# A two-part transformer on one core: attention heads emitted by pairs instead of one by one

## The chip, the cores and the metric

The kernel runs on one core of one Trainium2 chip. TensorE (PE) multiplies matrices into banks of PSUM, VectorE (DVE), ScalarE (ACT) and GpSimd (POOL) work element by element, SyncE (SP) issues the DMA of the weights. The metric is the device time of one execution in microseconds; lower is better. The kernel before took 1622.57 us, the median of three runs (1611.64 to 1628.34).

## The reference, cut to what matters

256 tokens of 1024 numbers go through two blocks. The first has two layers: differential attention and an expert layer of 64 experts, then multi-head latent attention and a second expert layer. The second block modulates, runs a hybrid mixer of two kinds of attention side by side, and a convolutional gated MLP. All is float32. The parts that the change touches:

```python
def mla_attention(...):                 # 8 heads; q and k of a head: 128 plain + 64 rotated numbers
    ...
    sc = einsum('bqhd,bkhd->bhqk', qb, k) * 192 ** -0.5      # plain part + rotated part
    p = causal_softmax(sc, blk, s)
    return einsum('bhqk,bkhd->bqhd', p, v)                   # v of a head: 128

def swa_attention(q, k, v, sinks):      # 8 window heads of 64, 2 heads of k and v
    scores = q k^T / 8 - slope(h) * dist, masked to a window of 128
    p = exp(scores - m);  probs = p / (sum(p) + exp(sink - m));  out = probs v

def forgetting_attention(q, k, v, f_logit):   # 8 heads of 64
    F = cumsum(log_sigmoid(f_logit))
    s = q k^T / 8 + (F[query] - F[key]);  p = softmax(causal(s));  out = p v
```

## The kernel before, in words

Tokens lie in two tiles of 128 partitions. Weights stream into 19 regions of 8 KB per partition by a plan that is worked off in a fixed order as regions come free (`Regions.fill`, SyncE's queue). Projections are made exact enough by splitting both operands into a rounded part and a rest (ScalarE L412, VectorE L413) and multiplying three times (`mm3`, L428 to L430); these operands are of the type that TensorE takes in one pass, while plain float32 matmuls appear in the trace as two records, one for each pass.

A head of attention has two stages. `stage_a`, `swa_a`, `fox_a` transpose q and k, multiply them into scores (a `sc` bank, of which there are two), and call `probs`: VectorE adds the mask or bias and takes row maxima (L599, L601), ScalarE exponentiates with row sums (L629), VectorE divides (L635, L637). `stage_b`, `swa_b`, `fox_b` call `probsT`, three transposes of the probabilities (L609) into an `at` bank (two of these) and a copy (L611), multiply with v, and split the result into `oT`. `staged(n, ...)` emits the stages of successive items interleaved; a `None` among the stages delays the next one by one item.

In the latent attention (L1281 to L1313) each head has four score matmuls: 128 and then 256 columns, each of them a product over all 128 rows (L1299, L1301) and one over the 64 rotated numbers (L1300, L1302). A pair of heads shares the transposed rotated parts in one tile `pq`, head c in partitions 64c to 64c+63; there is one `pq` for all pairs. A window head has two score matmuls over 64 rows (L1410, L1411). A forgetting head (`fox`) has its two (L1435, L1437), each followed by a bias matmul (L1436, L1438): a column of the identity over 8 rows, repeated to 128 columns, times the negated sums `nfT`. The values of window and forgetting heads come from `av` (L1397, L1398), 64 result partitions for each head, two heads in one bank.

The order on each engine comes from a scheduler that weighs what is ready; SyncE's is the program's. It puts weight matmuls of other projections (L428 to L430) between the heads' work: in the first half of the latent attention those of the second half, in the window heads those of q, k and v of the forgetting heads, in the forgetting heads the first part of the output projection (`out_proj`), all of which need VectorE and ScalarE for splits.

Of the kernel before, what the change touches and what calls it, by code (L numbers as in the profile page):

```python
# [19 lines left out]
P = 128  # L20
# [215 lines left out]
def tile_model(ctx: ExitStack, tc: tile.TileContext, a: dict, out: bass.AP, stop: int = 6):  # L236
# [39 lines left out]
    def phase(*shapes):  # L276

        room, o, out = sp.tile([P, 1152], F32, tag="phase", name="phase", bufs=1), 0, []
# [3 lines left out]
        assert o <= 1152  # L282
        return out
# [515 lines left out]
    def router_weights(i):  # L799

        room, = phase((1152,))
# [358 lines left out]
    def mla():  # L1160
# [35 lines left out]
        rt, kpe, pq = phase((2, T, 2, 64), (T, 64), (512,))  # L1196
# [19 lines left out]
        for i in range(2):  # L1216
# [64 lines left out]
            def stage_a(h, qp=qp, kp=kp, qn=qn, kn=kn, qs=qs, nqs=nqs):  # L1281
                if h % 2 == 0:
                    pt = at_ps()
                    for t in range(T):
                        PE.transpose(pt[:, ts(t, P)], qp[:, t, h:h + 2, :].rearrange("p a b -> p (a b)"), ident)
                        PE.transpose(pt[:, 256 + 128 * t:384 + 128 * t],
                                     kp[:, t, h:h + 2, :].rearrange("p a b -> p (a b)"), ident)
                    V.tensor_copy(pq, pt)
                pt = at_ps()
                for t in range(T):  # L1290
                    PE.transpose(pt[:, ts(t, P)], qn[:, t, h, :], ident)
                    PE.transpose(pt[:, 256 + 128 * t:384 + 128 * t], kn[:, t, h, :], ident)
                qT = t1((256,))
                kT = t1((256,))
                S.activation(qT, pt[:, 0:256], AF.Copy)
                V.tensor_scalar(kT, pt[:, 256:512], gqk[:, 0:1], None, op0=ALU.mult)
                ps = sc_ps()
                rsl = slice(64 * (h % 2), 64 * (h % 2) + 64)
# [6 lines left out]
            def stage_b(h, vv=vv, i=i):  # L1305
                pT = probsT(state[h])
                po = at_ps()
                PE.matmul(po[:, 0:256], lhsT=vv[:, 0, h, :], rhs=pT[:, 0:256], start=True, stop=False,
                          skip_group_check=True)
                PE.matmul(po[:, 128:256], lhsT=vv[:, 1, h, :], rhs=pT[:, 256:384], start=False, stop=True,  # L1310
                          skip_group_check=True)
                split_to(oT[0][:, 4 * i + h, :], oT[1][:, 4 * i + h, :], po[:, 0:256])
            staged(4, stage_a, None, stage_b)  # L1313
# [24 lines left out]
    def mixer():  # L1338
# [3 lines left out]
        kd, va, nfT = phase((T, 4, 64), (T, 2, 64), (256,))  # L1342
        nfT = nfT[0:8, :]
# [30 lines left out]
        PE.matmul(pf[:, 8:16], lhsT=ones, rhs=fl[:, 0, :], start=False, stop=True)  # L1374
        fc = sb([P, T, 8], "fc")
        V.tensor_copy(fc, pf[:, 0:16].rearrange("p (t h) -> p t h", t=2))
        pf2 = at_ps()
        for t in range(T):
            PE.transpose(pf2[0:8, ts(t, P)], fc[:, t, :], ident)
        V.tensor_scalar(nfT, pf2[0:8, 0:256], -8.0, None, op0=ALU.mult)  # L1380
# [14 lines left out]
        def av(po, c, v0, v1, pT):  # L1395
            rs_ = slice(64 * c, 64 * c + 64)
            PE.matmul(po[rs_, 0:256], lhsT=v0, rhs=pT[:, 0:256], start=True, stop=False, skip_group_check=True)  # L1397
            PE.matmul(po[rs_, 128:256], lhsT=v1, rhs=pT[:, 256:384], start=False, stop=True, skip_group_check=True)  # L1398

        def swa_a(h):  # L1400
            hp, c = divmod(h, 2)
            kv = hp // 2
            if h % 4 == 0:
                state["kT"] = pair_T(lambda t: kd[:, t, 2 * kv:2 * kv + 2, :].rearrange("p a b -> p (a b)"))
            if c == 0:
                state["qT"] = pair_T(lambda t: qa[:, t, ts(hp, P)])
            qT, kT = state["qT"], state["kT"]
            rsl = slice(64 * c, 64 * c + 64)
            ps = sc_ps()
            PE.matmul(ps[:, 0:128], lhsT=qT[rsl, 0:128], rhs=kT[rsl, 0:128], start=True, stop=True)  # L1410
            PE.matmul(ps[:, 128:384], lhsT=qT[rsl, 128:256], rhs=kT[rsl, 0:256], start=True, stop=True)  # L1411
            bias = t1((256,))
            G.tensor_scalar(bias, dist, -8.0 * 2.0 ** (-8.0 * (h + 1) / 8), None, op0=ALU.mult)
            state[h] = probs(ps, bias[:, 128:256], bias, 0.125, -0.125,
                             sink=bc("sinks", 8)[:, h:h + 1])

        def swa_b(h):
            hp, c = divmod(h, 2)
            if c == 0:
                state["po"] = at_ps()  # L1420
            pT = probsT(state[h])
            av(state["po"], c, va[:, 0, hp // 2, :], va[:, 1, hp // 2, :], pT)
            if c == 1:
                split_to(oT[0][:, hp, :], oT[1][:, hp, :], state["po"][:, 0:256])

        def fox_a(h):
            hp, c = divmod(h, 2)
            if c == 0:
                state["fqT"] = pair_T(lambda t: qb[:, t, ts(hp, P)])
                state["fkT"] = pair_T(lambda t: kb[:, t, ts(hp, P)])  # L1430
            qT, kT = state["fqT"], state["fkT"]
            rsl = slice(64 * c, 64 * c + 64)
            eh = ident[0:8, h:h + 1].to_broadcast([8, P])
            ps = sc_ps()
            PE.matmul(ps[:, 0:128], lhsT=qT[rsl, 0:128], rhs=kT[rsl, 0:128], start=True, stop=False)  # L1435
            PE.matmul(ps[:, 0:128], lhsT=eh, rhs=nfT[:, 0:128], start=False, stop=True)  # L1436
            PE.matmul(ps[:, 128:384], lhsT=qT[rsl, 128:256], rhs=kT[rsl, 0:256], start=True, stop=False)  # L1437
            PE.matmul(ps[:, 128:384], lhsT=eh, rhs=nfT[:, 0:256], start=False, stop=True)  # L1438

            state[h] = probs(ps, cmask, fmask, 0.125, -0.125)  # L1440

        def fox_b(h):
            hp, c = divmod(h, 2)
            if c == 0:
# [169 lines left out]
```

## Time and profile before

| | us |
|---|---|
| median of 3 runs | 1622.57 |
| lowest, highest | 1611.64, 1628.34 |
| profiled execution | 1618.73 |
| its span | 1616.9 |
| TensorE, VectorE, ScalarE busy in it | 1338.3, 690.5, 434.3 |
| heads of the latent attention, from | 686 to 744 |
| window heads | 1279.7 to 1324.1 |
| forgetting heads | 1339.7 to 1396.6 |

All prices are read from the one profiled execution. A matmul's shown duration contains time in which the next one already runs, so a price is the distance from one start to the next. [...]

### The profile page before, as it was taken

The page shows a single profiled execution, that of the slowest core. Times are in us where ns is not written, and L with a number is a line of the kernel's source. Part 1 is how long each engine was busy: PE and PEld are TensorE (multiplying, and loading weights), DVE is VectorE, ACT ScalarE, POOL GpSimd, SP SyncE. Part 2 cuts the span into 40 slices and gives each one's busy share as a digit, 9 for nine tenths or more (in the row PEclk, how much of TensorE's full clock was granted, in tenths as well). Part 3 has the DMA queues.
Part 4 walks back from the last instruction along what each step waited for, and adds up shares of the span by engine and source line. Part 5 has one row for each costly group of instructions (what it writes and reads, how often), then busy time and mean ns, then how long its engine had stood idle before and what let it go on. Part 6 is the DMA issues. An engine that isn't in the chain of part 4 may idle for free. (4 is left out here: it accounts for less than half of the span.)

```text
span 1616.9 us, 26717 instructions
## 1 busy us (share of the span) xinstructions
PE 1338.3 (83%) x10695; PEld 933.2 (58%) x10695; DVE 690.5 (43%) x1630; ACT 434.3 (27%) x946; POOL 53.5 (3%) x73
## 2 busy tenths in 40 slices
PE   7998987777677777998877777778785999999996
PEld 6766655544443444776644544545452666699996
DVE  6875232222222223875222222222323654477776
ACT  5754010000000001764000000000102443465554
POOL 2110000000000000110000000000000100000001
PEclk9998999898899988999989898898987998899998
DMA  9377889999999997227999999999899763575500
GB/s 365 124 301 326 348 352 417 419 419 417 419 419 418 418 419 295 92 107 314 393 418 418 418 419 418 418 419 388 348 419 368 266 228 114 177 256 180 176 34 27
DMA packets 109020, 513.03 MB, mean 317 GB/s; under 512 B 9875, under 2 KB 37331, under 8 KB 57552
## 3 DMA queue, kind: packets, MB, share of 16 engines
q1 hardware_dynamic: 107280, 507.42, 78.7%
q8 instruction: 160, 2.62, 0.7%
q0 software_dynamic: 1248, 2.00, 0.4%
q14 instruction: 108, 0.88, 0.1%
q10 hardware_dynamic: 224, 0.10, 0.0%
HBM read 508.43 MB, written 1.05 MB: 315 GB/s over the span
## 5 line engine op out<-in xcount | busy, mean ns | idle before, releaser
L981 PE MATMUL ad<-R,t 128*32 128x256 f32 x4096 | 299.1, 411 | 87.5 <-DMA R<-in_moe_w_up_dram 36.5
L981 PEld LDWEIGHTS ad<-R,t 128*32 128x32 f32 x4096 | 157.9, 118 | 233.3 <-issue 71.8
L936 PE MATMUL sc<-t,R 128*128 128x128 f32 x1024 | 169.4, 334 | 7.6 <-issue 7.4
L936 PEld LDWEIGHTS sc<-t,R 128*128 128x128 f32 x1024 | 161.4, 247 | 8.9 <-issue 8.2
L1031 DVE TENSOR_TENSOR x<-x,mm 128x512 f32<-128x512 f32 x140 | 90.0, 684 | 147.8 <-PE mm L1028 147.8
L987 ACT ACTIVATE t<-ad 128x256 f32<-128x256 f32 x32 | 12.3, 383 | 440.2 <-PE ad L981 440.2
L1008 PE MATMUL mm<-R,t 128*32 128x512 f32 x1024 | 120.0, 610 | 9.3 <-PEq L1072 5.9
L422 ACT ACTIVATE t<-mm,ws 128x512 fp32r<-128x512 f32 x64 | 44.0, 687 | 262.7 <-PE mm L1008 262.6
L413 DVE TENSOR_TENSOR R<-R,R 128x1024 fp32r<-128x1024 f32 (+3 forms) x78 | 90.9, 1169 | 33.5 <-ACT R L412 32.3
L989 DVE TENSOR_TENSOR t<-t,ad 128x256 f32<-128x256 f32 x32 | 13.5, 421 | 212.8 <-ACT t L987 212.8
L413 DVE TENSOR_TENSOR t<-R,t 128x1024 fp32r<-128x1024 f32 (+3 forms) x76 | 89.5, 1182 | 22.2 <-ACT t L412 22.0
L938 DVE TENSOR_TENSOR t<-sc,ffng 128x512 f32<-128x512 f32 x64 | 44.3, 692 | 126.9 <-PE sc L936 126.9
L960 PE MATMUL at<-con,t 128*128 128x128 f32 x64 | 16.0, 340 | 96.9 <-PEq L1108 90.3
L412 ACT ACTIVATE R<-R 128x1024 fp32r<-128x1024 f32 (+3 forms) x78 | 78.7, 1013 | 52.8 <-PE ad L430 20.2
L423 DVE SCALAR_TENSOR_TENSOR t<-mm,ws,t 128x512 fp32r<-128x512 f32 x64 | 48.1, 751 | 101.9 <-ACT t L422 75.1
L1028 PE MATMUL mm<-t,t 128*128 128x512 f32 x256 | 77.7, 423 | 11.1 <-DVE x L1031 10.2
L412 ACT ACTIVATE t<-R 128x1024 fp32r<-128x1024 f32 (+3 forms) x76 | 76.5, 1009 | 32.8 <-PE ad L429 13.2
L1008 PEld LDWEIGHTS mm<-R,t 128*32 128x32 f32 x1024 | 30.9, 112 | 73.6 <-issue 70.0
L960 PEld LDWEIGHTS at<-con,t 128*128 128x128 f32 x64 | 7.4, 162 | 110.3 <-issue 104.4
L1028 PEld LDWEIGHTS mm<-t,t 128*128 128x128 f32 x256 | 43.1, 188 | 45.2 <-DVE x L1031 22.9
L428 PE MATMUL mm<-R,R 128*128 128x512 f32 (+3 forms) x139 | 56.3, 408 | 2.6 <-ACT R L412 2.6
L429 PE MATMUL mm<-R,R 128*128 128x512 f32 (+3 forms) x139 | 55.9, 403 | 0.5 <-DVE R L413 0.5
(472 smaller groups left out, 2346.6 us busy)
## 6 DMA issues: line engine op xcount, KB each, us to landing
R<-in_moe_w_gate_dram SPq DMA_DIRECT2D x128, 1024.0 KB, 19.7
R<-in_moe_w_up_dram SPq DMA_DIRECT2D x128, 1024.0 KB, 18.8
R<-in_moe_w_down_dram SPq DMA_DIRECT2D x128, 1024.0 KB, 19.8
R<-in_w_ada_dram SPq DMA_DIRECT2D x24, 1024.0 KB, 7.7
R<-in_w_up_dram SPq DMA_DIRECT2D x22, 1024.0 KB, 6.2
R<-in_diff_w_in_dram SPq DMA_DIRECT2D x12, 1024.0 KB, 13.3
R<-in_w_down_dram SPq DMA_DIRECT2D x11, 1024.0 KB, 6.5
R<-in_w_in_dram SPq DMA_DIRECT2D x8, 1024.0 KB, 8.0
```

The lines of the kernel that those rows point to most:

```text
L412: S.activation(hi, w, AF.Copy)
L413: V.tensor_tensor(lo, w, hi.bitcast(F32), op=ALU.subtract)
L422: first = S.activation(hi, src, AF.Copy, scale=scale)
L423: V.scalar_tensor_tensor(lo, src, scale, hi.bitcast(F32), op0=ALU.mult, op1=ALU.subtract)
L428: PE.matmul(acc, lhsT=lt[0], rhs=rt[0], start=start, stop=False, **kw)
L429: PE.matmul(acc, lhsT=lt[0], rhs=rt[1], start=False, stop=False, **kw)
L936: PE.matmul(pg[:, ts(k4, P)], lhsT=h[:, t, 4 * hb + k4, :], rhs=gm[:, t].rearrange("p a b -> p (a b)"), start=(t == 0), stop=(t == 1))
L938: V.tensor_tensor(xg[hb], pg.rearrange("p (k n) -> p k n", k=4), gain[:, 4 * hb:4 * hb + 4, None].to_broadcast([P, 4, P]), op=ALU.mult)
L981: mm = PE.matmul(pgu[32 * j:32 * j + 32, co:co + 256], lhsT=xg[k // 4][:, k % 4, 32 * j:32 * j + 32], rhs=w, start=(k == 0 and co == 0), s ...
L1008: mm = PE.matmul(py[32 * j:32 * j + 32, :], lhsT=hT2[:, k, 32 * j:32 * j + 32], rhs=ws[j][:, k, ts(hf, 512)], start=(k == 0), stop=(k == 1))
L1028: PE.matmul(pos[t], lhsT=sc[:, ts(t, P)], rhs=y[part], start=(part == 0), stop=(part == 1))
L1031: V.tensor_tensor(xs, xs, pos[t], op=ALU.add)
```

## The change

Latent attention, window heads and forgetting heads go through `staged` by pairs of heads. A pair's scores are emitted column block by column block, both heads in turn, into two banks; the values likewise, both heads' 256 columns and then both heads' 128. In the latent attention the `None` between the stages is dropped, and `pq` is taken from a ring of slots for each pair. The sums of the forgetting bias are split into a rounded part and a rest, which stand in 16 rows of a one-pass type; the bias matmul multiplies them with a selector `e16` that has two ones in a column. The shared tile `phase` shrinks from 1152 to 768 numbers.

```diff
-            def stage_a(h, ...):
-                if h % 2 == 0:
-                    pt = at_ps()
...
-                    V.tensor_copy(pq, pt)
...
-                PE.matmul(ps[:, 0:128], lhsT=qT[:, 0:128], rhs=kT[:, 0:128], start=True, stop=False)
-                PE.matmul(ps[:, 0:128], lhsT=pq[rsl, 0:128], rhs=pq[rsl, 256:384], start=False, stop=True)
-                PE.matmul(ps[:, 128:384], lhsT=qT[:, 128:256], rhs=kT[:, 0:256], start=True, stop=False)
-                PE.matmul(ps[:, 128:384], lhsT=pq[rsl, 128:256], rhs=pq[rsl, 256:512], start=False, stop=True)
-                state[h] = probs(ps, cmask, fmask, qs[:, :, h], nqs[:, :, h])
+            def stage_a(hp, ...):
+                pq = t2((512,))
...
+                pss = [sc_ps(), sc_ps()]
+                for t, sl in QT:
+                    n = 128 * (t + 1)
+                    for c, (qT, kT) in enumerate(qk):
+                        PE.matmul(pss[c][:, sl], lhsT=qT[:, ts(t, P)], rhs=kT[:, 0:n], start=True, stop=False)
+                    for c in range(2):
+                        rsl = slice(64 * c, 64 * c + 64)
+                        PE.matmul(pss[c][:, sl], lhsT=pq[rsl, ts(t, P)], rhs=pq[rsl, 256:256 + n],
+                                  start=False, stop=True)
...
-            staged(4, stage_a, None, stage_b)
+            staged(2, stage_a, stage_b)
...
-        V.tensor_copy(fc, pf[:, 0:16].rearrange("p (t h) -> p t h", t=2))
+        V.tensor_scalar(fc, pf[:, 0:16].rearrange("p (t h) -> p t h", t=2), -8.0, None, op0=ALU.mult)
+        fhl = sb([P, T, 16], "fhl", 1, F32R)
+        split_to(fhl[:, :, 0:8], fhl[:, :, 8:16], fc)
...
+            PE.transpose(pf2[0:16, ts(t, P)], fhl[:, t, :].bitcast(F32), ident)
+        nfT = sb([16, 256], "nfT", 1, F32R)
+        V.tensor_copy(nfT, pf2[0:16, 0:256])
+        e16 = sb([16, 8], "e16", 1, F32R)
+        V.tensor_tensor(e16, ident[0:16, 0:8], ident[0:16, 8:16], op=ALU.add)
...
+        def scores(qT, kT, more=None):
+            pss = [sc_ps(), sc_ps()]
+            for t, sl in QT:
+                n = 128 * (t + 1)
+                for c in range(2):
+                    rsl = slice(64 * c, 64 * c + 64)
+                    PE.matmul(pss[c][:, sl], lhsT=qT[rsl, ts(t, P)], rhs=kT[rsl, 0:n], start=True, stop=more is None)
+                if more is not None:
+                    for c in range(2):
+                        more(pss[c][:, sl], c, n)
+            return pss
+        def av(hp, vs, k0):
+            pTs = [probsT(state[2 * hp + c]) for c in range(2)]
+            po = at_ps()
+            for c in range(2):
+                PE.matmul(po[64 * c:64 * c + 64, 0:256], lhsT=vs(c, 0), rhs=pTs[c][:, 0:256], start=True, stop=False,
+                          skip_group_check=True)
+            for c in range(2):
+                PE.matmul(po[64 * c:64 * c + 64, 128:256], lhsT=vs(c, 1), rhs=pTs[c][:, 256:384], start=False,
+                          stop=True, skip_group_check=True)
+            split_to(oT[0][:, k0 + hp, :], oT[1][:, k0 + hp, :], po[:, 0:256])
...
+            def forget(ps, c, n):
+                PE.matmul(ps, lhsT=e16[:, 2 * hp + c:2 * hp + c + 1].to_broadcast([16, P]), rhs=nfT[:, 0:n],
+                          start=False, stop=True)
...
-        staged(8, swa_a, None, swa_b)
+        staged(4, swa_a, None, swa_b)
...
-        staged(8, fox_a, None, fox_b)
+        staged(4, fox_a, None, fox_b)
```

How this moves the instructions is seen from the order that the scheduler gives. First TensorE's queue in the forgetting heads, at heads 2 and 3 before (`sc` is a score bank, `phase,con` are the sums and the identity, `t` the transposed q and k, the `at` rows of L609 transpose probabilities, those of L1397 and L1398 multiply values):

```order
L1435 MATMUL sc<-t_20758,t_20753 128x128
L1436 MATMUL sc<-phase,con 128x128
L1437 MATMUL sc<-t_20758,t_20753 128x256
L1438 MATMUL sc<-phase,con 128x256
L609 MATMUL at<-con,R_19856 128x128 x3
L1435 MATMUL sc<-t_20758,t_20753 128x128
L1436 MATMUL sc<-phase,con 128x128
L1437 MATMUL sc<-t_20758,t_20753 128x256
L1397 MATMUL at<-R_19857,R_19954 64x256
L1398 MATMUL at<-R_19857,R_19954 64x128
L1438 MATMUL sc<-phase,con 128x256
```

and the same pair now:

```order
L1417 MATMUL sc<-t_20756,t_20751 128x128 x2
L1451 MATMUL sc<-nfT,e_20146 128x128 x2
L1417 MATMUL sc<-t_20756,t_20751 128x256 x2
L1451 MATMUL sc<-nfT,e_20146 128x256 x2
L609 MATMUL at<-con,R_19856 128x128 x6
L430 MATMUL ad<-R_20946,R_20149 128x512
L1428 MATMUL at<-R_19857,R_19954 64x256 x2
L1431 MATMUL at<-R_19857,R_19954 64x128 x2
```

Both heads' matmuls of a kind stand next to each other, and the six transposes of the earlier pair follow, with one weight matmul before its values.

Second, TensorE's queue in the latent attention, at the scores of heads 0 and 1 before (the first of head 0's four, L1299, stands some rows earlier; `phase` is `pq`):

```order
L1300 MATMUL sc<-phase 128x128
L1301 MATMUL sc<-t_10588,t_10587 128x256
L1302 MATMUL sc<-phase 128x256
L1299 MATMUL sc<-t_10613,t_10612 128x128
L1300 MATMUL sc<-phase 128x128
L1301 MATMUL sc<-t_10613,t_10612 128x256
L1302 MATMUL sc<-phase 128x256
```

and now (L1304 over 128 rows, L1308 over 64):

```order
L1308 MATMUL sc<-R_10103 128x128
L1304 MATMUL sc<-t_10588,t_10587 128x256
L1304 MATMUL sc<-t_10597,t_10596 128x128
L1308 MATMUL sc<-R_10103 128x128
L1304 MATMUL sc<-t_10597,t_10596 128x256
L1308 MATMUL sc<-R_10103 128x256 x2
```

The scheduler leaves the 64-row matmuls of 128 columns apart and brings those of 256 columns together.

## Rows read from the trace of the kernel before

**Rows 1.** Busy time by stretch: length, busy us (records) of PE, PEld, DVE, ACT, POOL; clock, DMA share, GB/s.
```profile
686.00:744.00 58.00, 57.44 (x289) 43.00 (x290) 41.01 (x141) 36.50 (x118) 7.09 (x12) 1.00 0.34 133
1279.70:1324.10 44.40, 44.00 (x237) 25.59 (x235) 27.76 (x97) 21.04 (x59) 4.10 (x5) 1.00 0.54 196
1339.73:1396.60 56.87, 56.87 (x215) 35.90 (x213) 21.39 (x81) 20.23 (x51) 0.00 (x0) 0.82 0.20 66
```
**Rows 2.** TensorE's timeline, window heads 0 and 1 together, then 2 alone: start, length us.
```profile
1279.91 0.50 PE L1410 MATMUL sc<-t,t 64*128 64x128 f32 x4
...
1280.77 0.50 PE L430 MATMUL mm<-R,R 128*128 128x512 f32 x1
...
1290.34 0.48 PE L1410 MATMUL sc<-t,t 64*128 64x128 f32 x2
...
1291.19 0.55 PE L609 MATMUL at<-con,R 128*128 128x128 f32 x3
```
**Rows 3.** TensorE's timeline, a forgetting head's scores; another head's values.
```profile
1355.01 0.49 PE L1435 MATMUL sc<-t,t 64*128 64x128 f32 x2
1355.43 0.48 PE L1436 MATMUL sc<-phase,con 8*128 8x128 f32 x2
1355.84 0.70 PE L1437 MATMUL sc<-t,t 64*128 64x256 f32 x2
1356.47 0.69 PE L1438 MATMUL sc<-phase,con 8*128 8x256 f32 x2
1357.09 0.55 PE L609 MATMUL at<-con,R 128*128 128x128 f32 x3
...
1366.63 0.65 PE L1397 MATMUL at<-R,R 128*64 128x256 f32 x2
1367.12 0.38 PE L1398 MATMUL at<-R,R 128*64 128x128 f32 x2
1367.43 0.44 PE L1390 MATMUL at<-con,R 128*128 128x128 f32 x2
```
**Rows 4.** TensorE's timeline, latent heads: one matmul among full ones; a whole head.
```profile
689.27 0.38 PE L1299 MATMUL sc<-t,t 128*128 128x128 f32 x2
689.49 0.27 PE L1291 MATMUL at<-con,R 128*128 128x128 f32 x1
...
702.48 0.49 PE L1299 MATMUL sc<-t,t 128*128 128x128 f32 x2
702.90 0.48 PE L1300 MATMUL sc<-phase 64*128 64x128 f32 x2
703.31 0.70 PE L1301 MATMUL sc<-t,t 128*128 128x256 f32 x2
...
704.57 0.70 PE L1308 MATMUL at<-R,R 128*128 128x256 f32 x2
```
**Rows 5.** Weight matmuls: two in TensorE's timeline; groups by line, their loads.
```profile
1267.42 0.39 PE L429 MATMUL mm<-R,R 128*128 128x512 f32 x1
1267.65 0.39 PE L430 MATMUL mm<-R,R 128*128 128x512 f32 x1
...
L429 PEld LDWEIGHTS mm<-R,R 128*128 128x128 f32 x139 | 27.7, 199 | 7.2 <-DVE R L413 1.8 <-issue 1.6
```
**Rows 6.** TensorE's timeline, tiles of 32 columns in the second expert layer.
```profile
912.29 3.64 PE L981 MATMUL ad<-R,t 128*32 128x256 f32 x58 [1.85 <-DMA R<-in_moe_w_up_dram]
```
**Rows 7.** Busy time by stretch, the three of the forgetting stage at half clock.
```profile
1344.87:1351.72 6.85, 6.85 (x18) 4.35 (x18) 2.28 (x12) 2.90 (x8) 0.00 (x0) 0.51 0.39 124
1358.69:1365.11 6.42, 6.42 (x15) 3.82 (x15) 2.45 (x12) 2.24 (x9) 0.00 (x0) 0.50 0.00 0
1385.85:1392.26 6.41, 6.41 (x18) 4.12 (x16) 1.58 (x9) 1.09 (x4) 0.00 (x0) 0.50 0.01 3
```
**Rows 8.** Timelines of TensorE and VectorE, end of the first window pair's softmax.
```profile
1284.73 0.61 PE L609 MATMUL at<-con,R 128*128 128x128 f32 x3 [0.40 <-DVE R L637]
...
1285.36 0.55 DVE L637 TENSOR_SCALAR R<-R,at_l 128x128 f32<-128x128 f32 x2
```

More of the change, by code (lines that the diff above doesn't have):

```diff
@@ L276, in phase @@
     def phase(*shapes):
-        room, o, out = sp.tile([P, 1152], F32, tag="phase", name="phase", bufs=1), 0, []
+        room, o, out = sp.tile([P, 768], F32, tag="phase", name="phase", bufs=1), 0, []
         for shape in shapes:
@@ L799, in router_weights @@
     def router_weights(i):
-        room, = phase((1152,))
+        room, = phase((768,))
         wr = view(room[:, 144:], (8, 72))
@@ L1279, in mla, with stage_a @@
                 reg.give(ra0, ra1)
-            def stage_a(h, qp=qp, kp=kp, qn=qn, kn=kn, qs=qs, nqs=nqs):
-                if h % 2 == 0:
+            def stage_a(hp, qp=qp, kp=kp, qn=qn, kn=kn, qs=qs, nqs=nqs):
+                pq = t2((512,))
+                pt = at_ps()
+                for t in range(T):
+                    PE.transpose(pt[:, ts(t, P)], qp[:, t, 2 * hp:2 * hp + 2, :].rearrange("p a b -> p (a b)"), ident)
+                    PE.transpose(pt[:, 256 + 128 * t:384 + 128 * t],
+                                 kp[:, t, 2 * hp:2 * hp + 2, :].rearrange("p a b -> p (a b)"), ident)
+                V.tensor_copy(pq, pt)
+                qk = []
+                for h in (2 * hp, 2 * hp + 1):
@@ new lines, in stage_b @@
+            def stage_b(hp, vv=vv, i=i):
+                for h in (2 * hp, 2 * hp + 1):
+                    pT = probsT(state[h])
+                    po = at_ps()
+                    PE.matmul(po[:, 0:256], lhsT=vv[:, 0, h, :], rhs=pT[:, 0:256], start=True, stop=False,
+                              skip_group_check=True)
+                    PE.matmul(po[:, 128:256], lhsT=vv[:, 1, h, :], rhs=pT[:, 256:384], start=False, stop=True,
+                              skip_group_check=True)
+                    split_to(oT[0][:, 4 * i + h, :], oT[1][:, 4 * i + h, :], po[:, 0:256])
@@ L1393, in pair_T @@
             return dst
[L1395 to L1401, printed above, removed]
+        def scores(qT, kT, more=None):
[9 more added lines that the diff above has]
+            return pss
@@ new lines, in av @@
+        def av(hp, vs, k0):
+            pTs = [probsT(state[2 * hp + c]) for c in range(2)]
+            po = at_ps()
+            for c in range(2):
+                PE.matmul(po[64 * c:64 * c + 64, 0:256], lhsT=vs(c, 0), rhs=pTs[c][:, 0:256], start=True, stop=False,
+                          skip_group_check=True)
+            for c in range(2):
+                PE.matmul(po[64 * c:64 * c + 64, 128:256], lhsT=vs(c, 1), rhs=pTs[c][:, 256:384], start=False,
+                          stop=True, skip_group_check=True)
+            split_to(oT[0][:, k0 + hp, :], oT[1][:, k0 + hp, :], po[:, 0:256])
@@ L1402, in swa_a @@
+        def swa_a(hp):
             kv = hp // 2
-            if h % 4 == 0:
+            if hp % 2 == 0:
                 state["kT"] = pair_T(lambda t: kd[:, t, 2 * kv:2 * kv + 2, :].rearrange("p a b -> p (a b)"))
[L1405 to L1440, printed above, removed]
@@ L1442, in fox_b @@
-        def fox_b(h):
-            hp, c = divmod(h, 2)
-            if c == 0:
-                state["po"] = at_ps()
-            pT = probsT(state[h])
-            av(state["po"], c, vb[:, 0, ts(h, 64)], vb[:, 1, ts(h, 64)], pT)
-            if c == 1:
-                split_to(oT[0][:, 4 + hp, :], oT[1][:, 4 + hp, :], state["po"][:, 0:256])
-        staged(8, swa_a, None, swa_b)
+            pss = scores(pair_T(lambda t: qa[:, t, ts(hp, P)]), state["kT"])
+            for c in range(2):
+                h = 2 * hp + c
+                bias = t1((256,))
+                G.tensor_scalar(bias, dist, -8.0 * 2.0 ** (-8.0 * (h + 1) / 8), None, op0=ALU.mult)
+                state[h] = probs(pss[c], bias[:, 128:256], bias, 0.125, -0.125, sink=bc("sinks", 8)[:, h:h + 1])
@@ new lines, in swa_b, with fox_a @@
+        def swa_b(hp):
+            av(hp, lambda c, t: va[:, t, hp // 2, :], 0)
+        def fox_a(hp):
+            def forget(ps, c, n):
+                PE.matmul(ps, lhsT=e16[:, 2 * hp + c:2 * hp + c + 1].to_broadcast([16, P]), rhs=nfT[:, 0:n],
+                          start=False, stop=True)
+            pss = scores(pair_T(lambda t: qb[:, t, ts(hp, P)]), pair_T(lambda t: kb[:, t, ts(hp, P)]), forget)
+            for c in range(2):
+                state[2 * hp + c] = probs(pss[c], cmask, fmask, 0.125, -0.125)
```

40 lines of the change are left out of this document (14 added, 26 removed).

## The prediction

> **What bounds the kernel now.** I read the busy time by stretch first [rows 1]. In the latent attention's heads (686 to 744 us) TensorE is busy 57.44 of 58.00 us, in the window heads (1279.70 to 1324.10) 44.00 of 44.40, in the forgetting heads (1339.73 to 1396.60) all 56.87. VectorE and ScalarE are busy 27.76 and 21.04 of the 44.40 us, and the DMA share is 0.34, 0.54 and 0.20. So in these stretches time taken from TensorE's queue shortens the run, unless something new makes TensorE wait. The same rows give the granted clock: 1.00 in the first two, 0.82 in the third.
>
> Next TensorE's timeline, to price the kinds of matmul from start to start. A window head alone takes 0.85 us: its matmuls on 64 rows start at 1290.34, the next work at 1291.19. The first two window heads, which the scheduler had put behind each other, take 0.86 us for both, 1279.91 to 1280.77 [rows 2]. Two heads whose operands lie in partitions 0 to 63 and 64 to 127 and whose scores go to two banks thus run side by side. A forgetting head takes 2.08 us: 0.42 and 0.63 for its own two matmuls, 0.41 and 0.62 for the two bias matmuls of 8 rows; its values take 0.80, 0.49 and 0.31 [rows 3]. A latent head takes 2.09 us, and a full 128-column matmul there 0.42, but 0.22 where other full ones follow (689.27): each turn between full and 64 rows costs some 0.2 us [rows 4]. Weight matmuls of 512 columns, one pass each, follow each other at 0.23 us, although each loads weights for 0.199 [rows 5]. Tiles of 32 columns run four at a time in the experts: 58 records, 29 matmuls of two passes, in 3.64 us are 0.126 us each [rows 6], where a value matmul of as many moving columns takes 0.49 [rows 3].
>
> [...]
>
> **The change, part by part.** Terms at full clock; G is one of the weight matmuls of 0.23 us that the scheduler strews between heads; counts of G are from the order.
>
> Forgetting scores. Four bias matmuls of a pair, two passes each on 8 rows, become four of one pass on 16 rows, and the two heads' own matmuls stand together. The own ones then cost a pair 0.42 + 0.63 = 1.05 us [rows 2, 3]. The bias: 256 columns at half of a G is 0.12 us, 128 columns between 0.06 and 0.12; I take 0.12 for all four, since the weights they load are as wide, and 0.1 for each of two turns of mode more: 0.68 [rows 4, 5]. A pair goes from 4.16 to 1.73 us; four pairs: **-9.7**. The ends: bias at nothing, -12.4; heads not side by side, -5.5.
>
> [...]
>
> Values. Where the four matmuls of a pair stand together, their heads, which write to partitions 0 to 63 and 64 to 127, should go side by side as the experts' tiles do [rows 6]: 0.80 instead of 1.60 us. The order has three such pairs in the forgetting stage and two in the window stage; in the other three the 256-column matmuls are apart and only the short ones, 0.31, meet. 5 x 0.8 + 3 x 0.3: **-4.9** (2.7 and 2.2). The ends: 0 and -6.4.
>
> Window scores. The first pair was side by side already, the second is parted by a G, the third and fourth come together: 2 x 0.85 [rows 2], **-1.7**.
>
> Latent scores. The matmuls of 256 columns on 64 rows meet, the short ones stay apart, and eight turns of mode become six: 4 x 0.42 + 0.43 + 0.63 + 0.63 = 3.37 against 4.18 us a pair [rows 4]; four pairs: **-3.2**. The ends: 0, and -7.4 if all 64-row matmuls meet.
>
> These sum to -19.5.
>
> New waits. [...] The first window pair is the measure: its scores end at 1280.77, TensorE stands 0.40 us for the first head until 1284.73, and the second head's last division ends at 1285.91 [rows 2, 8]: 4.0 and 5.1 us. In the forgetting stage, between a pair's scores and its transposes, now stand the earlier pair's transposes and values, the next q and k with 8 G, and the next scores: over 5 us, so that chain is covered. What stays is a stand of some 0.5 us, the copy of the transposed probabilities, before each pair's values, with one G to fill it: **+2.0**. In the window stage the first pair has 8 G, two lone heads' scores and a head's transposes, 4.2 us, before its second head at 5.1; the third has values, 4 G, scores and two transposes, 3.2 us, before its first head at 4.0: **+1.7**. In the latent attention the empty step between the two stages is gone: behind a pair's scores stand 14, 16, 12 and 11 G, 2.5 to 3.7 us, against 4.0 for the first head: 0.8 + 0.3 + 1.2 + 1.5, **+3.8**, which eats the gain there. The ends for all twelve pairs: 0 and 12 x 1.5 = +18.
>
> The clock. Three stands at half cost 0.49 x 6.85 + 0.5 x 6.42 + 0.5 x 6.41 = 9.8 us [rows 7]. What went before them, 4.2 us of score matmuls, shrinks to 1.73 us a pair. In the latent and window heads, where 64-row matmuls stand among full ones, the clock stayed at 1.00 [rows 1]. So I take all three as gone: **-9.8**. The ends: that, and +3.3 for one more.
>
> Costed at nothing: the split of the sums into two parts, their transposes, the selector and the copy of pq into the slot ring, which end long before their readers, behind G's; without that cover about 1 us each. DMA: its queue keeps its order, the loads wait for the same last readers, which come earlier, and at shares of 0.20 to 0.54 there is room [rows 1].
>
> Sum: -19.5 + 7.5 - 9.8 = **-21.8**. The profiled execution took 1618.7 us (span 1616.9), so 1596.9 by it. That execution lies 3.8 under the median of the runs shown, 1622.6, whose ends are 1611.6 and 1628.3; by the median it is 1600.8. I forecast 1599.
>
> **The rivals.**
> 1. The clock still falls. For it: transposes and short bias passes stand in a row now, and why it fell is inferred from three places. Against: the 8-row matmuls are what these places have and the two stages at 1.00 lack. Then -12.0: about 1609, with one or two falls in between.
> 2. Slower: the softmax of pairs sets the time. Both heads go through VectorE and ScalarE at once; if other work in those queues stretches the second head's chain from 5.1 to 8 us, each of twelve pairs waits some 3 us at its transposes: +36 - 19.5, and with the clock as before 1635. It decides from 1.6 us a pair. For it: the latent attention has lost its empty step, and 57 G stand behind the last forgetting values instead of 18, so less is left to fill with. Against: VectorE is busy 41.01 of 58.00 us at most, and a forgetting pair asks 21.39 / 4 = 5.3 us of VectorE and 5.1 of ScalarE [rows 1], where TensorE has some 6 (1.73, 0.80, 8 G and ten transposes). [...]
> 3. The tiles do not meet as hoped: no values side by side, and no more scores than did already. Then the bias alone, -5.5, waits of +4 and the clock -9.8: -11.3, about 1609. Against it: [rows 2, 6].
> 4. The saved time is lost again, to weights that come late or waits between stages that were hidden: 1610 to 1620. Against it: the shares of DMA.
>
> **How the numbers follow.** Forecast 0.56, rival 1 0.22, rival 2 0.06, rival 3 0.09, rival 4 0.07. The forecast's own spread, from the ends of single terms, is 1588 to 1607. The range leaves out rival 2 and the outer ends: 1584 to 1615. One per cent, about what can be told from no change, is 16 us: under 1606 is faster. The forecast lies there nearly whole, rivals 1 and 3 to a third: faster 0.62, within 1% 0.32, slower 0.06.
>
> **What would show it.** Right: a forgetting pair's scores take 1.6 to 1.9 us and four value matmuls 0.8; the clock is 1.00 through the forgetting stage, which from the first transposes to the last values takes some 28 instead of 56.87 us, with 39 more G behind it (9 us); the window stage is 2 us shorter, the latent one as long as before with waits of 3 to 4 us. Wrong: waits for VectorE at the probability transposes above 1.6 us a pair, 64-column matmuls that follow at 0.49 us each, or a clock near 0.8 in that stage.

## The result, and the profile after

The changed kernel takes **1604.31 us** (median of 7 runs, 1595.07 to 1606.46) against 1622.57 of the kernel before: ratio 0.9876, 95% interval 0.9853 to 0.9900. Forecast were 1599 us, in a range of 1584 to 1615. The profiled execution took 1605.11 us, span 1603.3.

Where the time went is read from stretches. The first fence is the kernel before, the second the changed one: busy time by stretch, for the latent attention with its projections, from the first window scores to the first forgetting transposes, and from there to the end of the output projection.

```profile
652.11:751.77 99.66, 97.49 (x510) 78.34 (x509) 73.22 (x216) 64.65 (x205) 11.61 (x16) 1.00 0.36 133
1279.91:1339.73 59.82, 59.42 (x330) 37.52 (x330) 35.19 (x111) 26.18 (x66) 4.78 (x6) 1.00 0.62 224
1339.73:1402.66 62.93, 62.93 (x237) 39.95 (x235) 23.70 (x85) 22.87 (x55) 0.00 (x0) 0.84 0.26 84
```
```profile
654.43:753.14 98.71, 95.14 (x510) 77.74 (x509) 72.96 (x216) 64.37 (x206) 12.23 (x16) 1.00 0.33 124
1288.63:1344.98 56.35, 55.21 (x326) 34.71 (x326) 32.47 (x111) 26.14 (x66) 4.78 (x6) 1.00 0.66 238
1344.98:1387.73 42.75, 42.64 (x222) 29.38 (x220) 23.21 (x86) 21.54 (x55) 0.00 (x0) 1.00 0.60 203
```

The forgetting stretch lost 20.18 us, and its granted clock, the share of the full one that the rows show, is 1.00 throughout where it was 0.84; from the first transposes to the last values it is 27.7 us (some 28 forecast); the window stretch lost 3.47, while the projections ahead of it took 1.3 longer; the latent stage lost 0.95. From the mixer's first transposes to the MLP's first it is 158.47 before and 136.13 after, -22.3. The profiled spans differ by 13.6 only: the two expert layers, whose code is the same, took 2.6 and 6.0 us longer in this execution, the rest 1.1. The medians differ by 18.3.

TensorE's timeline of the changed kernel (start, length): a forgetting pair's scores up to the next work; its values; a window pair's values; a latent pair's scores up to the next work.

```profile
1346.47 0.49 PE L1417 MATMUL sc<-t,t 64*128 64x128 f32 x4
1346.89 0.43 PE L1451 MATMUL sc<-nfT,e 16*128 16x128 f32 x2
1347.26 0.70 PE L1417 MATMUL sc<-t,t 64*128 64x256 f32 x4
1347.89 0.49 PE L1451 MATMUL sc<-nfT,e 16*128 16x256 f32 x2
1348.31 0.44 PE L1405 MATMUL at<-con,R 128*128 128x128 f32 x2
...
1353.50 0.81 PE L1428 MATMUL at<-R,R 128*64 128x256 f32 x3
1353.98 0.38 PE L1431 MATMUL at<-R,R 128*64 128x128 f32 x2
1354.14 0.38 PE L1428 MATMUL at<-R,R 128*64 128x256 f32 x1
1354.36 0.38 PE L1431 MATMUL at<-R,R 128*64 128x128 f32 x2
1354.67 0.44 PE L1405 MATMUL at<-con,R 128*128 128x128 f32 x2
...
1298.68 0.65 PE L1428 MATMUL at<-R,phase 128*64 128x256 f32 x4
1299.16 0.39 PE L1431 MATMUL at<-R,phase 128*64 128x128 f32 x4
1299.48 0.44 PE L1405 MATMUL at<-con,phase 128*128 128x128 f32 x2
...
707.94 0.38 PE L1304 MATMUL sc<-t,t 128*128 128x128 f32 x2
...
710.56 0.70 PE L1308 MATMUL sc<-R 64*128 64x256 f32 x4
711.19 0.44 PE L429 MATMUL mm<-t,R 128*128 128x384 f32 x1
```

A forgetting pair's scores take 1346.47 to 1348.31, 1.84 us, where two heads took 4.16 [rows 3]: own matmuls of both heads side by side in 0.42 and 0.63, two bias matmuls in 0.37 and 0.42. A window pair's four value matmuls take 0.80, as one head's did [rows 3]. The forgetting ones take 1.17, and TensorE's weight loads there tell why:

```profile
1353.49 0.19 PEld L1428 LDWEIGHTS at<-R,R 128*64 128x64 f32 x2 [0.33 <-ACT R L611]
1353.88 0.13 PEld L1428 LDWEIGHTS at<-R,R 128*64 128x64 f32 x1 [0.19 <-ACT R L611]
```

Each head's values wait for its own copy of the transposed probabilities (line 611), and both copies stand behind each other on ScalarE. The second head starts 0.4 us late, beside the first one's short matmul. The latent pair takes 3.25 us.

### The profile page after: what moved, and what is told of

It reads as the page before. It is cut to its first block, busy times and chain, and to the rows that moved or that the text cites. A ratio compares the mean times of both kernels' runs of the same rounds, so it can differ in the third digit from the quotient of the medians.

```text
span 1603.3 us, 26694 instructions
## 1 busy us (share of the span) xinstructions
PE 1319.4 (82%) x10679; PEld 917.0 (57%) x10679; DVE 687.4 (43%) x1632; ACT 432.4 (27%) x947; POOL 54.4 (3%) x73
## 5 line engine op out<-in xcount | busy, mean ns | idle before, releaser
L981 PE MATMUL ad<-R,t 128*32 128x256 f32 x4096 | 313.3, 426 | 94.7 <-DMA R<-in_moe_w_up_dram 35.3
L981 PEld LDWEIGHTS ad<-R,t 128*32 128x32 f32 x4096 | 163.5, 121 | 248.5 <-issue 85.9
L936 PE MATMUL sc<-t,R 128*128 128x128 f32 x1024 | 161.2, 323 | 8.1 <-issue 7.9
L936 PEld LDWEIGHTS sc<-t,R 128*128 128x128 f32 x1024 | 153.0, 236 | 9.2 <-issue 8.7
L960 PEld LDWEIGHTS at<-con,t 128*128 128x128 f32 x64 | 7.2, 158 | 105.6 <-issue 99.7
L428 PE MATMUL mm<-R,R 128*128 128x512 f32 (+3 forms) x139 | 55.6, 403 | 2.7 <-ACT R L412 2.6
L428 PE MATMUL mm<-t,R 128*128 128x512 f32 (+3 forms) x139 | 54.2, 391 | 1.0 <-DVE R L594 0.8
```

The lines of the kernel that those rows point to most:

```text
L428: PE.matmul(acc, lhsT=lt[0], rhs=rt[0], start=start, stop=False, **kw)
L936: PE.matmul(pg[:, ts(k4, P)], lhsT=h[:, t, 4 * hb + k4, :], rhs=gm[:, t].rearrange("p a b -> p (a b)"), start=(t == 0), stop=(t == 1))
L981: mm = PE.matmul(pgu[32 * j:32 * j + 32, co:co + 256], lhsT=xg[k // 4][:, k % 4, 32 * j:32 * j + 32], rhs=w, start=(k == 0 and co == 0), s ...
```

## The experiments

"Forgetting stretch" is that of the third row above; "mixer" is from its first transposes to the MLP's first (158.47 before, 136.13 changed), "latent stage" the first row (99.66 and 98.71). Ratios are to the kernel before.

**The bias alone** (before, with the one-pass bias; the only other edit is pq):

```
-            eh = ident[0:8, h:h + 1].to_broadcast([8, P])
+            eh = e16[:, h:h + 1].to_broadcast([16, P])
...
-        rt, kpe, pq = phase((2, T, 2, 64), (T, 64), (512,))
+        rt, kpe = phase((2, T, 2, 64), (T, 64))
+                    pq = state["pq"] = t2((512,))
```

> The kernel before with the one-pass bias of 16 rows alone: heads still come one by one, values too (the latent attention keeps its order; its rope tile pq only lies in the slot ring, as in the change, to make room). Stretch measured: first transposes of the forgetting heads to the end of the output projection, 62.93 us before, 42.75 after. Theory A: the clock falls came from the two-pass bias matmuls on 8 rows. Then a head's scores go from 2.08 to about 1.55 us (8 x -0.5 = -4.2) and the three half-clock stands of 9.8 us are gone: stretch about 49 us, run about -14. Rival B: the falls came from long stretches of 64-row scores of single heads, and only the pairs end them: the stands stay, stretch about 58.7 us, run about -4.

Measured: 1622.69 us, ratio 0.9998 (0.9975 to 1.0022), yet the mixer is 149.66, 8.8 shorter, and the forgetting stretch 53.49. A head's scores take 1.60 us (1354.61 to 1356.21). Both theories miss on the clock: two shorter stands at half clock (0.51 and 0.50) remain.

```profile
1356.28:1359.73 3.45, 3.45 (x9) 2.65 (x10) 2.15 (x11) 1.29 (x6) 0.00 (x0) 0.51 0.86 275
1380.24:1383.67 3.43, 3.43 (x10) 2.39 (x9) 1.93 (x10) 2.21 (x9) 0.00 (x0) 0.50 0.00 0
```

3.4 us lost at half clock instead of 9.8, and 8 x 0.48 = 3.8 by shorter matmuls: together 10.2, of which 8.8 show. The run's time hardly moved because the latent stage is 107.97, 8.3 longer; why is taken up below.

**The pairs alone** (changed kernel, old bias):

```
-                PE.matmul(ps, lhsT=e16[:, 2 * hp + c:2 * hp + c + 1].to_broadcast([16, P]), rhs=nfT[:, 0:n],
+                PE.matmul(ps, lhsT=ident[0:8, 2 * hp + c:2 * hp + c + 1].to_broadcast([8, P]), rhs=nfT[:, 0:n],
```

> The changed kernel, with the old two-pass fp32 bias over 8 rows in the pairs' scores: pairs alone. A pair's scores then take 1.05 + 4 two-pass bias matmuls (2.06) = 3.1 us instead of 1.84: four pairs, +5.1 us against the change. Theory A (the 8-row bias makes the clock fall): one to three stands of some 6.5 us at half clock come back, +3.3 to +9.8 more: stretch from the first forgetting transposes to the end of the output projection 51 to 58 us. Rival B (pairs end the falls): clock 1.00 throughout, stretch 47.8 us.

Measured: 1604.26 us, ratio 0.9881 (0.9851 to 0.9911). A pair's scores take 2.75 us (1346.76 to 1349.51), less than the 3.1 expected; the stretch is 48.33, with one short stand:

```profile
1354.18:1357.61 3.43, 3.43 (x11) 2.14 (x11) 2.16 (x14) 2.61 (x10) 0.00 (x0) 0.50 0.03 7
```

Between the two theories: pairs remove two of three stands, not all. Of the 5.6 us by which the stretch is longer than the changed kernel's, 4 x 0.91 = 3.6 are bias matmuls and 1.7 the stand.

**The rows of the bias** (before, with the same two-pass bias over all partitions):

```
-        nfT = nfT[0:8, :]
+        V.memset(nfT, 0.0)
...
-            eh = ident[0:8, h:h + 1].to_broadcast([8, P])
+            eh = ident[:, h:h + 1].to_broadcast([P, P])
```

> The kernel before, its fp32 bias in two passes over all 128 rows instead of 8 (rows 8 to 127 are zeros). The columns that pass are as many, so a bias matmul should still take 0.41 and 0.62 us. If it is the few rows at work that let the clock fall (theory A, its finer form): clock 1.00 through the forgetting heads, stretch to the end of the output projection 62.9 - 9.8 = 53 us. If it falls for another reason (what stands in the queue there, whatever the rows): three stands at half clock stay, 62.9 us.

Measured: 1618.03 us in one run; the stretch took 52.75 us at a clock of 1.00, 10.2 less than before.

```profile
1361.26 0.48 PE L1435 MATMUL sc<-t,t 64*128 64x128 f32 x2
1361.67 0.49 PE L1436 MATMUL sc<-phase,con 128*128 128x128 f32 x2
1362.09 0.70 PE L1437 MATMUL sc<-t,t 64*128 64x256 f32 x2
1362.72 0.70 PE L1438 MATMUL sc<-phase,con 128*128 128x256 f32 x2
...
1349.16:1401.91 52.75, 52.75 (x237) 35.09 (x235) 23.59 (x85) 22.98 (x55) 0.00 (x0) 1.00 0.31 101
```

The bias matmuls last 0.42 and 0.63 as before [rows 3]; only the rows that work are more, and every stand is gone. So by this run the falls came from the few rows, 8 at a clock of 0.84 and 128 at 1.00, though TensorE was busy all the time, 62.93 of 62.93 us and 52.75 of 52.75. This is one execution; the three stands of before were seen in two.

**Values head by head** (changed kernel):

```
                 PE.matmul(po[64 * c:64 * c + 64, 0:256], lhsT=vs(c, 0), rhs=pTs[c][:, 0:256], start=True, stop=False,
                           skip_group_check=True)
-            for c in range(2):
                 PE.matmul(po[64 * c:64 * c + 64, 128:256], lhsT=vs(c, 1), rhs=pTs[c][:, 256:384], start=False,
```

> The changed kernel, but a pair's four value matmuls go head by head (256 and 128 columns of the first head, then of the second) and not in turn. If two tiles go side by side only where they are neighbours in the queue, just the first head's short one meets the second head's long one: 0.49 + 0.49 + 0.31 = 1.3 us a pair instead of 0.80, eight pairs, +4 us. If neighbourhood in the queue isn't needed (the second head's pair overtakes or the whole block overlaps), 0.80 stays. If nothing meets, 1.60, +6.4 us.

Measured: 1602.59 us in one run, stretch 42.96 (+0.2), mixer 136.6. In the first window pairs TensorE's queue holds 256, 128, 256, 128 columns, and yet the timeline shows:

```profile
1295.15 0.66 PE L1428 MATMUL at<-R,phase 128*64 128x256 f32 x4
1295.63 0.40 PE L1430 MATMUL at<-R,phase 128*64 128x128 f32 x4
1295.96 0.44 PE L1405 MATMUL at<-con,phase 128*128 128x128 f32 x2
```

0.81 us: the second head's long matmul, whose results go to the other 64 partitions, starts with the first head's long one, ahead of the short one queued before it. The change's order within the four is worth nothing here, 0.81 us against 0.80; that nothing full stands between them is what counts: in the changed kernel the third and fourth window pairs have weight matmuls between the heads and take 0.57 us ahead of these and 0.80 behind them.

**The latent attention as before** (changed kernel, old heads and empty step, pq in the slot ring):

> The changed kernel with the latent attention of before (heads one by one, the empty step between the stages; its rope tile from the slot ring as in the change). If the latent part is worth next to nothing, as forecast (-3.2 +3.8) and as its stage shows (100.55 to 99.60 us), the run is within 2 us of the change, and the second expert layer (496.7 us before, 502.7 after) is as long as in any other run, by chance. Rival: the new latent order made the second expert layer 6 us longer; then that layer is back at some 497 us and the run is 5 us faster than the change.

Measured: 1605.97 us, ratio 0.9894 (0.9850 to 0.9938); second expert layer 502.4 us, mixer 135.63, latent stage 104.93. The expert layer's 503.6 us in the changed kernel is thus not the latent order's work; over the profiled runs that layer took 497 to 508. The stage is 6.2 us longer, but that is not what the pairs are worth there. Here too pq lies in the ring, and VectorE's and TensorE's timelines show a wait for the router's weights of the next layer:

```profile
729.27 0.76 DVE L822 TENSOR_TENSOR phase<-phase,vT 128x576 f32<-128x576 f32 x1 [5.41 <-DMA phase<-in_moe_w_expert_dram]
731.78 0.33 PE L609 MATMUL at<-con,R 128*128 128x128 f32 x1 [3.53 <-DVE R L637]
```

Behind it the clock stands at half for 3.4 us. The run with only pq moved, below, keeps the old heads as well and has the same stage, 104.92. Without the wait and the stand, 104.93 - 3.53 - 1.7 = 99.7 us are left by estimate, 1 us more than the changed kernel's.

**The empty step back** (`staged(2, stage_a, None, stage_b)`):

> The changed kernel with an empty step between scores and values of the latent attention's pairs (as the heads had it before). Theory: the waits of TensorE for the pairs' softmax there (2.0 us idle in the stage, against 0.56 before) are due to the dropped step: they fall to under 1 us and the stage is 1 to 1.5 us shorter. Rival: with only two pairs in a group the filler runs out all the same, behind the second pair, and the waits stay at 2 us.

Measured: 1604.99 us, ratio 0.9895 (0.9850 to 0.9940), latent stage 102.06 with 3.9 us of TensorE idle. Neither theory: the wait behind the dropped step goes, others come, and the stage is 3.4 us longer. Only half of that is the empty step's. The rows are this latent stage, then that of the run with the values head by head, whose latent attention is the changed kernel's:

```profile
653.00:755.06 102.06, 98.18 (x510) 79.81 (x509) 72.63 (x216) 63.87 (x205) 12.94 (x16) 0.98 0.41 157
652.40:752.75 100.35, 96.81 (x511) 79.04 (x510) 72.99 (x216) 64.26 (x205) 12.47 (x16) 0.98 0.33 121
```

Both contain a half-clock stand of 3.4 us at some 687 us, as the heads begin; the profiled execution of the changed kernel has none there. Against the second row the empty step costs 1.7 us.

**Fewer turns, and fewer turns with the empty step**:

```
                     for c, (qT, kT) in enumerate(qk):
                         PE.matmul(pss[c][:, sl], lhsT=qT[:, ts(t, P)], rhs=kT[:, 0:n], start=True, stop=False,
+                                  skip_group_check=True)
+                for t, sl in QT:
+                    n = 128 * (t + 1)
                     for c in range(2):
...
-                if more is not None:
-                    for c in range(2):
-                        more(pss[c][:, sl], c, n)
+            if more is not None:
+                for t, sl in QT:
+                    for c in range(2):
+                        more(pss[c][:, sl], c, 128 * (t + 1))
```

> The changed kernel with fewer turns of kind: in a latent pair the four full-row matmuls come first, then the four on 64 rows (2 turns instead of 6, or 8 before), and in a forgetting pair the four own ones first, then the four bias ones (2 turns instead of 4). At 0.2 us a latent turn 4 x 4 x 0.2 = 3.2 us less, at 0.1 us a forgetting one 4 x 2 x 0.1 = 0.8: a latent pair's scores at 2.4 us instead of 3.25, a forgetting pair's at 1.65 instead of 1.84, run -4 against the change. Rival: in the latent attention the saved time turns into waits for the softmax, since less stands behind the scores: then the stage is less than 1 us shorter.

> Both of the last two: the changed kernel with the fewer turns and the empty step in the latent attention. If waits eat what the latent scores gain, the empty step gives it back: latent stage 3 to 5 us shorter than in the change, run -4 to -6 against it. If the empty step doesn't help, as the run with fewer turns alone.

In these two kernels the second block of a bank has a start flag of its own behind the first block's product and ahead of the additions to both, and the output is off by a relative 0.98. That the first block's own product is what they leave out of the scores is the author's estimate; no run shows it by itself. The matmuls are as many, and only their times are used. Measured: 1604.01 us (0.9837 to 0.9931 of before) and 1605.50 (0.9844 to 0.9934). A forgetting pair's scores fell to 1.51 us and the stretch to 41.39, -1.36 where -0.8 was expected. The latent part failed: the stage is 102.43, since the scheduler put three of the four pairs apart again (one took 2.26 us), and a wait came that nobody had counted. VectorE's timeline with the fewer turns:

```profile
727.88 0.76 DVE L822 TENSOR_TENSOR phase<-phase,vT 128x576 f32<-128x576 f32 x1 [4.18 <-DMA phase<-in_moe_w_expert_dram]
```

The scaling of the router's weights for the next layer stands in VectorE's queue among the heads' softmax and waits 4.18 us for its load; a division behind it holds TensorE for 3.9 us, and its clock falls to 0.50 for some 6.8 us. With the empty step as well it is 3.38 and 2.6 us and the stage 100.29, still 1.6 longer than the changed kernel's, so that step doesn't help the run. The run with the bias alone has the same row with 5.67 us, and 3.8 us of TensorE.

**Only pq moved** (before):

```
-        rt, kpe, pq = phase((2, T, 2, 64), (T, 64), (512,))
+        rt, kpe = phase((2, T, 2, 64), (T, 64))
...
+                    pq = state["pq"] = t2((512,))
```

> The kernel before with one edit: the latent attention's rope tile pq lies in the slot ring, as the change has it, and no longer in the tile called phase. It frees phase earlier, and the product of the router's weights for the second expert layer (line 822), which writes phase, moves 36 places up in VectorE's queue. Theory: this is why the one-pass bias alone (1622.69 us) showed next to nothing in the time although the mixer was 8.8 us shorter. VectorE then waits 5 to 6 us there for the weights, TensorE 3.5 to 3.8 us for a division behind it, and its clock falls to half behind that for some 7 us (another 3.5): latent stage 105 to 108 us instead of 99.7, run +5 to +8 against before. Rival: the place of pq is worth nothing, latent stage near 100, run within 2 us of before, and the old forgetting stage simply varies. Its forgetting heads are those of before: a second look at them, three half-clock stands expected.

Measured: 1627.41 us, ratio 1.0045 (1.0030 to 1.0059), by the ratio +7.3 us; latent stage 104.92, +5.3, with a half-clock stand of 3.4 us where 7 were expected. POOL's, VectorE's and TensorE's timelines of this kernel, then POOL's and VectorE's of before and of the changed one:

```profile
720.16 0.88 POOL L804 DMA_DIRECT2D phase<-in_moe_w_expert_dram  x1
729.01 0.76 DVE L822 TENSOR_TENSOR phase<-phase,vT 128x576 f32<-128x576 f32 x1 [5.65 <-DMA phase<-in_moe_w_expert_dram]
731.52 0.43 PE L609 MATMUL at<-con,R 128*128 128x128 f32 x1 [3.77 <-DVE R L637]
```
```profile
739.61 0.88 POOL L804 DMA_DIRECT2D phase<-in_moe_w_expert_dram  x1
743.06 0.76 DVE L822 TENSOR_TENSOR phase<-phase,vT 128x576 f32<-128x576 f32 x1 [0.71 <-DMA phase<-in_moe_w_expert_dram]
```
```profile
718.59 0.88 POOL L804 DMA_DIRECT2D phase<-in_moe_w_expert_dram  x1
723.72 0.75 DVE L822 TENSOR_TENSOR phase<-phase,vT 128x576 f32<-128x576 f32 x1
```

While pq lay in phase, the next use of that tile, the router's weights, could not load before the last pair's scores. In the ring it loads 19 us earlier, and the product moves with it to where a wait stops the softmax. In the changed kernel it stands there too, but the load landed in time. SyncE's queue shows what goes with this, first in this kernel, then in the changed one:

```profile
717.63 2.08 SPq L123 DMA_DIRECT2D R<-in_moe_w_gate_dram  x4
719.62 2.21 SPq L123 DMA_DIRECT2D R<-in_moe_w_gate_dram  x4
```

These four belong to a burst of seven weight loads of 1 MB. In this kernel GpSimd's 256 KB, issued at 720.16, come behind six of them; in the changed one, issued at 718.59, they come ahead of all. In all ten profiled executions that issue the load near this burst it goes the same way: behind five or more of the seven, the reader starts 8.0 to 8.9 us after the issue and has waited 1.5 to 5.7; ahead of them, at most 5.3 us after it, without a wait. No run turned that order alone. The old forgetting stretch, seen a second time, is 62.89 us at 0.84, with its three stands: they are no chance of one execution.

**The bias alone, the product late again**:

```
+                if i == 1 and h == 3:
+                    V.tensor_tensor(sb([P, 1], "late"), kpe[:, 0, 0:1], ps[:, 0:1], op=ALU.add)
```

> The run with the one-pass bias alone (pq in the slot ring), plus one 4-byte operation behind the last latent scores that reads phase, so that the router's product stands as late in VectorE's queue as before. Theory: the 3.8 us wait and the clock fall in the latent heads go, latent stage 100 to 101 us instead of 108.0; the forgetting stretch stays at 59 us; run -9 against before, -7 against the one without this operation. Rival: the bias alone is worth nothing in the run's time: as that run, -2.

Measured: 1616.85 us, ratio 0.9964 (0.9948 to 0.9980), by the ratio -5.8 us; latent stage 101.17, the product at 747.52, forgetting stretch 54.92 (the 59 expected runs on to the end of the mixer). The theory holds in kind and by the place, while the size is smaller. In the profiled execution the second stand in the forgetting heads lasted 6.82 us and the mixer is 151.6; but that execution, 1624.37, was the slowest of seven, so why the median gains less than 9 us isn't shown.

**The second head's copy on VectorE**:

```
-            pTs = [probsT(state[2 * hp + c]) for c in range(2)]
+            pTs = [probsT(state[2 * hp + c], c == 1) for c in range(2)]
```

> The changed kernel with the second head's transposed probabilities copied by VectorE, the first's still by ScalarE (mixer only). Theory: in the forgetting heads the second head's values start 0.43 us after the first's because both copies stand in ScalarE's queue, so a pair's values take 1.17 us instead of 0.80. Then 0.8 to 0.9, three pairs, about -1 us in the stretch from the first forgetting transposes to the end of the output projection (42.75). Rival: VectorE, with the other pair's softmax in its queue, copies later than ScalarE: values at 1.2 us or more and the stretch longer.

Measured: 1600.20 us, ratio 0.9865 (0.9849 to 0.9882); the stretch is 43.66, 0.9 longer. The rival: in a pair of the forgetting stage the first head's values start at 1353.69, the second's at 1355.16, with weight matmuls between them.

**The three together** (turns with one start flag a bank, late reader, copy):

```
-                        PE.matmul(pss[c][:, sl], lhsT=qT[:, ts(t, P)], rhs=kT[:, 0:n], start=True, stop=False)
+                        PE.matmul(pss[c][:, sl], lhsT=qT[:, ts(t, P)], rhs=kT[:, 0:n], start=t == 0, stop=False,
+                                  skip_group_check=True)
```

> The changed kernel with three edits together: fewer turns of kind in the pairs' scores (as before in the run with fewer turns, now with one start flag for each bank, the rest as additions into it), the late reader of phase, and the second head's copy by VectorE. A forgetting pair's scores 1.51 instead of 1.84 us (as that run had), its values 0.8 to 0.9 instead of 1.17, one latent pair 1 us shorter; no wait for the router's product and no clock fall in the latent heads: mixer 136.1 - 2.3 = 133.8 us, latent stage 98, run -3 against the change, about 1601 us. Rival: the waits and expert layers swallow it: 1604.

Measured: **1594.08 us** (1591.10 to 1594.69, 4 runs), ratio 0.9825 (0.9809 to 0.9842): faster than the kernel before and, by intervals that don't overlap (on another chip), than the changed one. Busy time of its latent stage, mixer and forgetting stretch:

```profile
654.38:751.96 97.58, 95.38 (x510) 78.02 (x509) 73.34 (x217) 64.45 (x205) 12.56 (x16) 0.98 0.36 134
...
1249.16:1382.77 133.61, 131.66 (x782) 88.13 (x783) 85.06 (x259) 64.34 (x150) 8.30 (x10) 0.99 0.66 235
1335.32:1377.61 42.29, 42.27 (x222) 28.62 (x220) 24.90 (x90) 20.51 (x51) 0.00 (x0) 1.00 0.53 178
```

The stages edited give 1.1 and 2.5 us against the changed kernel, as forecast, although the latent stage's 0.98 is again a half-clock stand at some 689 us, as the heads begin. The run gained some 10 us where 3 were forecast. The profiled executions differ by 10.6; of the rest 6.4 lie in the second expert layer, whose code is the same, and no run here says why. Since the copy by itself lengthened the stretch, the gain is put down to the turns and the late product, though they were not run without it.

## Why the prediction was right, point by point

- **Forgetting scores, -9.7**: measured 4 x (4.16 - 1.84) = -9.3. The bias cost 0.79 a pair where 0.68 was taken. The 0.68 was an estimate from the rows of loads and matmuls [rows 4, 5].
- **Values, -4.9**: 0.80 a pair where both copies were ready, two in the window stage. In the forgetting stage three pairs took 1.17, -1.3 instead of -2.4. Here the step was mis-sized: the half microsecond for the copy had been put ahead of a pair's values, and lay in part between the two heads.
- **Window scores, -1.7**: the pairs stood as read from the order, one side by side as before, one parted, two new at 0.85. Waits there were 0.82 and 0.18 against 0.40 before, +0.6 instead of +1.7.
- **Latent scores, -3.2, and waits, +3.8**: a pair took 3.25 (3.37 forecast), -3.7 in four if the first, which a weight matmul parts, is counted alike. TensorE idled 3.57 us in the stage against 2.17 before, +1.4 instead of +3.8: the waits were over-priced. These two alone give -2.3; the stage lost 0.95. So the sign differs from the forecast's +0.6, by 1.6 us. Both stages are of executions without the half-clock stand at 687 to 692 us that seven of the 14 profiled executions have there, whatever the heads' order; with it the same latent attention takes 100.3.
- **Clock, -9.8**: all three stands went, in this execution and in the seven of the later kernels that keep both parts. Before, two heads' scores begin at 1341.19, 1355.01 and 1381.45 us of TensorE's timeline, and the stands, 6.4 to 6.9 us at 0.50 or 0.51, at 1344.87, 1358.69 and 1385.85 [rows 7]. The reason given, the 8-row matmuls in long rows of scores, is half the story as the runs tell it: 128 rows at work end the stands (1.00) with bias matmuls as long as before; on 16 rows in one pass, heads one by one, two remain (3.4 us each, or 3.4 and 6.8); in pairs on 8 rows one (3.4). The change needed both parts. Rival 1, that the clock still falls, would have come true in part for either half. One premise was weaker than it looked: the 1.00 in the latent heads was that execution's (see the point above).
- **"Costed at nothing ... the copy of pq into the slot ring"**: wrong as a step, and it fell out of the sum by luck. The copy itself costs nothing, but the tile it leaves lets a load and VectorE's product of the next layer go ahead: 7.3 us where that is the only edit, 5.3 of them in the latent stage. In the changed kernel the product meets a load that has landed. This is the mechanism of rival 4 (weights that come late), at a place that it had not named. Reading VectorE's order for what moves past the softmax, and POOL's for the load, would have shown it.
- **The sum** for the mixer, -22.4, was measured at -22.3. That it agrees so closely is luck in part: the values gave some 3.6 us instead of 4.9 and the projections ahead took 1.3 longer, which no term had foreseen, while the waits, taken as what is left, cost some 0.8 instead of 3.7. The expert layers' spread, some 5 us either way between executions, is what separates 1596.9 from the 1605.1 profiled; in the execution that the forecast started from both were near their shortest (509.5 and 497.6 us, where others took up to 515 and 508).

By the pieces, the bias alone comes to 0.9964 (with its side effect taken away), the pairs alone 0.9881, both 0.9876: the last two can't be told apart by the run's time, though the stretch shows 5.6 us between them.

## What to carry to other kernels

Where a tile leaves a shared buffer, ask what the buffer's next owner will do earlier, and which queue it will then stand in: here one operation of 4 bytes per partition that kept the buffer taken brought the latent stage from 107.97 to 101.17 us (the run from 0.9998 to 0.9964, intervals that still touch). Small matmuls are to be priced by the rows they put to work as well as by columns: here the same columns over 128 rows instead of 8 took the stretch from 62.93 to 52.75 us, at a clock of 1.00 instead of 0.84. To put two heads side by side, keep full matmuls from between them and see that both operands are ready: a pair's values took 0.80 us so, 0.57 and 0.80 around weight matmuls, 1.17 with the second copy late. The order among the four value matmuls mattered little, 0.81 against 0.80.

## What the runs showed of the hardware that was not expected

- The granted clock fell to 0.50 with TensorE busy all the time [rows 7]: the stretch is 62.93 us at 0.84 with bias matmuls on 8 rows, 52.75 at 1.00 with the same columns on 128 rows.
- A value matmul with results in the other 64 partitions started ahead of one queued before it: four matmuls queued as 256, 128, 256, 128 columns ran in 0.81 us as two pairs, the long ones from 1295.15, the short ones from 1295.63.
- A 256 KB load issued 720.16 us into the span kept its reader waiting until 729.01; issued at 718.59 in the changed kernel, its reader started at 723.72 without a wait. The first was issued behind six of SyncE's seven loads of 1 MB, the second ahead of them; this fits all ten profiled executions that issue it near that burst, though no run changed it alone.
